# All eight experts in unsplit float32 on quarters of TensorE's columns, with the split buffers as landing buffers

## The chip, the cores and the metric

The kernel runs on one core of one Trainium2 chip. The metric is device time in microseconds of one execution. Three runs of the kernel before gave 3044.08 (median), 3042.06 and 3046.80.

## The reference, cut to what matters

A layered network over 256 tokens of width 1024, all in float32: two transformer layers (attention mixers, then a dense feed-forward in the first and a mixture of experts in the second), and behind them two more layers of another form. The change touches the mixture of experts alone:

```python
logits = xt @ w_router                     # 256 tokens, 8 experts
top_v, top_e = lax.top_k(logits, 2)        # each token goes to two experts
gates = softmax(top_v)
for e in range(8):                         # on the tokens routed to e
    y[e] = (silu(x @ w1[e]) * (x @ w3[e])) @ w2[e]     # w1, w3: 1024 x 3584, w2: 3584 x 1024
out[token] += gate * y[e][token]
```

So there are 512 token slots in all. With the reference's own inputs the experts get 78, 76, 73, 69, 66, 64, 45 and 41 of them. The weights of one expert are 44 MB, of all eight 352.3 MB, and every one is read.

## The kernel before, in words

The program has three stages on one time line: the first layers (two half-batches of 128 tokens as two interleaved threads, `run_pair`), the experts (`moe`), and the last layers (`run_pair` again). All weights come through one `Stream`: a list of loads in order of use, issued by the SP queue (`load`, L333) into raw buffers of 8 KB a partition, of which there are `RAW_BUFS` = 5. A load is one megabyte, 128 partitions by 8 KB.

Float32 matmuls are made of three faster ones. Each half of a raw buffer is split (`need`): ScalarE rounds it to the matmul's fast format (`wh`, L369), VectorE writes the remainder (`wl`, L370), each into one of `SPLIT_BUFS` = 5 buffers of 4 KB; once both halves of the raw buffer are split it is free and the next load may be issued (`free`). `Thread.gemm` then issues for each 128 rows `xh*wh`, `xh*wl` and `xl*wh` (L420 to L422), with 128 tokens stationary and 512 weight columns moving.

Experts are ranked by their token count while the kernel runs; the five largest (`BIG`) get 128 slots and this split form (`expert128`). The three smaller ones get 64 slots and go unsplit (`expert64`, `gemm_pair`, L439): the array's columns are taken as four quarters of 32, two for the slots' two halves with one weight chunk (`w1`) and two with another (`w3`), so that the four quarters work side by side on raw float32 buffers. Such a matmul is two instructions in the trace. A smaller expert's load consists of two pieces of half a megabyte, one from each weight. The two sequences run merged (`run_merged`): units of smaller experts are spread between those of larger ones, from the twelfth load of the stage to the twentieth before its end.

The inner columns of an expert go in seven blocks of 512. Per block, the activation (ScalarE) and the product (VectorE) give `h`, which PE transposes some units later (`defer`, `Tplain` or `T`) into the stationary operand of the last product. That one's output `y` is split in two parts and scattered back to token order by matmuls with a one-hot matrix (`scp`), and `add_rows` (L1621) adds it to the residual with the gate's weight on VectorE. The rows of the next expert are fetched by an indirect DMA on the POOL queue (`gather`, `gather64`) by a side generator that makes a step every second unit. Behind the last expert come statistics (L1626) and the norm.

The first load of an expert can't be issued before routing has written its number to a register (`routing`, `reg`). `overflow` is a branch that is entered only where an expert has more tokens than its slots; it then reads all weights again. The order of instructions on each engine is made by a scheduler from priorities and dependencies, save where the kernel asks for program order.

Of the kernel before, what the change touches and what calls it, by code (L numbers as in the profile page):

```python
# [37 lines left out]
GATHER_AT = 3  # L38
GATHER_AT64 = 2
GATHER_WAIT = 8  # L40
# [7 lines left out]
SMALL_FROM = 12  # L48
SMALL_TO = 20
SPLIT_LEAD = 2.0  # L50
# [85 lines left out]
def weight_plan():  # L136
# [13 lines left out]
    for i in range(2):  # L150
# [17 lines left out]
        if i == 0:  # L168
            for ci, (a, b) in enumerate(chunks(2816)):
                add(("f1", ci), "dense_w1", (0,), a, b)  # L170
                add(("f3", ci), "dense_w3", (0,), a, b)
            full("f2", "dense_w2", (0,), D)
        else:
            for e in range(8):
                for ci in range(7):
                    add((e, "e1", ci), "expert_w1", (0, e), ci * 512, ci * 512 + 512)
                    add((e, "e3", ci), "expert_w3", (0, e), ci * 512, ci * 512 + 512)
                full((e, "e2"), "expert_w2", (0, e), D)
# [26 lines left out]
def weight_groups(shapes):  # L205

    out = []
    end = {}  # L210
    for key, name, idx, c0, c1 in weight_plan():
        kc = shapes[name][-2] // P
# [12 lines left out]
def packed_weights(h):  # L225
# [3 lines left out]
    for key, name, idx, c0, n, kc, groups in plan:  # L229
# [4 lines left out]
    return packs  # L234


def chunk_loads(name, n, kc, groups):
# [3 lines left out]
    for at, k, rows in groups:  # L241
        units = [(kk, min(per, rows - kk), k + kk, n, kc, kk + per >= rows) for kk in range(0, rows, per)]
        out.append(([(name, at, rows, 0, rows, n)], units))
    return out


def pair_loads(chunks):

    out = []
    kc = chunks[0][2]  # L250
    for g, (_, k, rows) in enumerate(chunks[0][3]):
        for j in range(0, rows, 2):
            out.append(([(name, gr[g][0], rows, j, 2, n) for name, n, _, gr in chunks],
                        [(None, 2, k + j, 512, kc, True)]))
    return out


class Stream:


    def __init__(self, m):
# [7 lines left out]
        self.owed = 0  # L269
        self.hold = None  # L270
# [8 lines left out]
    def add(self, key, name, n, kc, groups):  # L279
        assert key not in self.index  # L280
        for pieces, units in chunk_loads(name, n, kc, groups):
            self.loads.append((pieces, None))
            for u in units:
                self.unit(key, len(self.loads) - 1, *u)

    def add_experts(self, one):

        big, small = [], []
        for r in range(8):
            if r < BIG:  # L290
                for k, (name, n, kc, groups) in one.items():
                    big += [((r,) + k, r, pieces, units) for pieces, units in chunk_loads(name, n, kc, groups)]
            else:
                for ci in range(8):
                    ab = [one["e1", ci], one["e3", ci]] if ci < 7 else [one["e2", 0], one["e2", 1]]
                    small += [((r, ci), r, pieces, units) for pieces, units in pair_loads(ab)]
        step = (len(big) - SMALL_FROM - SMALL_TO) / len(small)
        work, load = [], []
        for i, x in enumerate(big):
            load.append((i - SPLIT_LEAD, x))  # L300
            work += [(i + j / len(x[3]), x, u) for j, u in enumerate(x[3])]
        for i, x in enumerate(small):
            load.append((SMALL_FROM + i * step, x))
            work += [(SMALL_FROM + i * step, x, u) for u in x[3]]
        li = {}
        for _, x in sorted(load, key=lambda a: a[0]):
            li[id(x)] = len(self.loads)
            self.loads.append((x[2], x[1]))
        self.hold = len(self.splits) + 1
        for _, x, u in sorted(work, key=lambda a: a[0]):  # L310
            self.unit(x[0], li[id(x)], *u)

    def load(self, parts=1):
        if self.next_load == len(self.loads):
            return
        li = self.next_load
        pieces, rank = self.loads[li]
        if rank is not None and rank not in self.m.expert:
            self.owed += 1
            return  # L320
        self.next_load += 1
        r = self.m.praw.tile([P, 2048], F32, name="raw", tag="raw")
        for i, (name, at, rows, j0, lk, n) in enumerate(pieces):
            v = r[:, i * lk * n:(i + 1) * lk * n].rearrange("p (k n) -> p k n", k=lk)
            if rank is None:
                src = self.m.I[name][at:at + P * rows * n].rearrange("(p k n) -> p k n", p=P, k=rows)
            else:
                w = self.m.I[name].rearrange("(e q) -> e q", e=8)
                src = w[bass.ds(self.m.expert[rank], 1), at:at + P * rows * n].rearrange(
                    "a (p k n) -> p (a k) n", p=P, k=rows)  # L330
            q = lk // parts
            for j in range(0, lk, q):
                self.m.nc.sync.dma_start(v[:, j:j + q], src[:, j0 + j:j0 + j + q])  # L333
        self.raw[li] = r if len(pieces) > 1 else v

    def pay(self):
        n, self.owed = self.owed, 0
        for _ in range(n):
            self.load()

    def start(self):
        for _ in range(RAW_BUFS - 1):
            self.load()
# [8 lines left out]
    def need(self, idx):  # L352
        m = self.m
        nc = m.nc
        while self.next_split <= min(idx, len(self.splits) - 1):
# [5 lines left out]
            if li not in self.raw or j == self.hold:  # L361
# [18 lines left out]
    def free(self, li):  # L380
        del self.raw[li]
        self.load()


class Thread:
# [40 lines left out]
    def gemm_pair(self, key, xT):  # L426

        m = self.m
        ps = m.aux(name="pair")
        for s in m.stream.index[key]:  # L430
            yield s
            li, _, sk, k0, n, kc, _ = m.stream.splits[s]
            w = m.stream.raw[li].rearrange("p (c k n) -> p c k n", c=2, k=sk)
            for j in range(sk):
                k = k0 + j
                x = xT(k)
                for c, h in ((1, 0), (1, 1), (0, 0), (0, 1)):
                    p = c * 64 + h * 32
                    i = m.nc.tensor.matmul(ps[p:p + 32, :n], x[:, h * 32:h * 32 + 32], w[:, c, j, :], start=(k == 0),  # L439
                                           stop=(k == kc - 1))  # L440
                    m.tc.keep_in_program_order(i)
            m.stream.free(li)
            self.tick()
        return ps
# [7 lines left out]
class Model:  # L452
# [115 lines left out]
    def run_merged(self, gens):  # L568

        cur = [next(g, None) for g in gens]  # L570
        while any(c is not None for c in cur):
            i = min((c, i) for i, c in enumerate(cur) if c is not None)[1]
            self.stream.need(self.stream.ahead(cur[i], SPLIT_BUFS - 2))
            self.stream.next_use = cur[i] + 1
            self.side_tick()
            cur[i] = next(gens[i], None)

# [81 lines left out]
    def Tplain(self, src, cols, width, dst, on_act):  # L659
# [3 lines left out]
        for j, c in enumerate(cols):  # L663
            nc.tensor.transpose(tp[:width, j, :], c, self.ident)  # L664
# [15 lines left out]
    def plan(self):  # L680
        S = self.stream = Stream(self)
        self.expert = {}
        one = {}
        for key, name, idx, c0, n, kc, groups in weight_groups(SHAPES)[0]:
            if not name.startswith("expert_"):
                S.add(key, name, n, kc, groups)
            elif idx[1] == 0:
                one[key[1:] if key[1] in ("e1", "e3") else ("e2", key[1])] = (name, n, kc, groups)
                if ("e2", 1) in one:
                    S.add_experts(one)  # L690


    def setup(self):
# [18 lines left out]
        self.stream.start()  # L712
# [9 lines left out]
    def setup_side(self):  # L722
# [95 lines left out]
        for j in range(3):  # L818
# [4 lines left out]
            self.dpart.append(d)  # L823
        yield
# [587 lines left out]
    def routing(self):  # L1412
# [48 lines left out]
        reg(0)  # L1461
        self.stream.pay()
        for r in range(BIG, 8):
            reg(r)
        for r in range(1, BIG):
            reg(r)
# [22 lines left out]
        nc.vector.tensor_scalar(out=cr[:, :BIG], in0=cr[:, :BIG], scalar1=-64.0, scalar2=None, op0=OP.add)  # L1489
# [5 lines left out]
        yield from self.gather(0)  # L1495
        self.stream.hold = None
# [7 lines left out]
    def gather(self, r):  # L1504
# [3 lines left out]
        s = self.st([P, 2, P], name="oh")  # L1508
        self.onehot(s, self.iota, lambda t: self.rtab[:, 0, t, r:r + 1], lambda t: self.rtab[:, 1, t, r:r + 1])
        yield  # L1510
        tp = self.aux((P, 4, P), name="ohp")
        for t in range(2):
            nc.tensor.transpose(tp[:, t, :], s[:, t, :], self.ident)
        sT = self.kvt([P, 2, P], F32R, name="ohT")
        xg = []
        if r == 0:
            gp = []
            for c in range(2):
                p = self.aux((P, 4, P), name="gp")
                for j in range(4):  # L1520
                    k = c * 4 + j
                    for t in range(2):
# [635 lines left out]
```

## Time and profile before

| | |
|---|---|
| median of the runs | 3044.08 us |
| the profiled execution | 3046.54 us |
| its span, first to last instruction | 3044.5 us |
| PE, VectorE, ScalarE busy in the span | 2949.0, 1957.1, 1533.4 us |
| bytes read from memory | 716.87 MB |

The profile's slices are fortieths of the span, 76 us each, with the busy share of each engine in tenths; PE's share comes from modelled ends and is no measure of its peak. The span's last instruction is the output's store, and the time of the execution lies 2.0 us above the span.

### The profile page before, as it was taken

How to read it: one execution, taken by the hardware profiler on the slowest of the kernel's cores; microseconds unless marked ns; L12 is line 12 of the kernel's file. 1: busy time of each engine (PE TensorE's matmuls, PEld its weight loads, DVE VectorE, ACT ScalarE, POOL GpSimd, SP SyncE). 2: the span in 40 equal slices, each digit the busy share in tenths (PEclk: the TensorE clock that was granted, in tenths of full speed). 3: DMA queues.
4: the chain of work that ended last, by engine and by line, in shares of the span. 5: the costliest groups of instructions: out<-in, count | busy, mean ns of one | idle time of the engine just before them, and what ended most of it. 6: DMA issues, size and time to landing. Idle time of an engine off the chain costs nothing. (4 is left out here: it accounts for less than half of the span.)

```text
span 3044.5 us, 40303 instructions
## 1 busy us (share of the span) xinstructions
PE 2949.0 (97%) x15216; PEld 2234.7 (73%) x15216; DVE 1957.1 (64%) x3240; ACT 1533.4 (50%) x2161; POOL 28.4 (1%) x47
## 2 busy tenths in 40 slices
PE   8999999999999999999999899999999999999998
PEld 6887887888655555555555688888888888888887
DVE  6877555777765565656555865757865655668655
ACT  4665444664654444544444644564454444654543
POOL 0000000000000000000000000000000000000000
PEclk9999999999999999999999999999999999999999
DMA  6445555442999999999999855545555555555552
GB/s 226 164 156 185 181 180 172 165 157 87 359 369 367 366 382 369 356 388 367 370 379 375 332 194 180 198 164 183 178 182 190 184 182 194 180 172 175 181 192 97
DMA packets 123048, 721.65 MB, mean 237 GB/s; under 512 B 13976, under 2 KB 14240, under 8 KB 55904
## 3 DMA queue, kind: packets, MB, share of 16 engines
q1 hardware_dynamic: 118368, 703.54, 63.6%
q0 software_dynamic: 4480, 15.48, 1.5%
q8 instruction: 121, 1.98, 0.3%
q14 instruction: 79, 0.65, 0.1%
HBM read 716.87 MB, written 2.10 MB: 236 GB/s over the span
## 5 line engine op out<-in xcount | busy, mean ns | idle before, releaser
L370 DVE TENSOR_TENSOR wl<-raw,wh 128x1024 fp32r<-128x1024 f32 (+1 forms) x1088 | 1299.8, 1215 | 689.9 <-ACT wh L369 686.5
L369 ACT CAST wh<-raw 128x1024 fp32r<-128x1024 f32 (+1 forms) x1088 | 1113.1, 1045 | 849.7 <-PE mm L422 709.4
L420 PE MATMUL mm<-wh,tg 128*128 128x512 f32 (+2 forms) x2928 | 1144.6, 391 | 1.5 <-ACT wh L369 1.0
L421 PE MATMUL mm<-wl,tg 128*128 128x512 f32 (+2 forms) x2928 | 1124.3, 384 | 15.3 <-DVE wl L370 15.0
L422 PE MATMUL mm<-wh,tg 128*128 128x512 f32 (+2 forms) x2928 | 1126.2, 385 | 0.0
L422 PEld LDWEIGHTS mm<-wh,tg 128*128 128x128 f32 x2928 | 552.1, 189 | 131.6 <-issue 24.3
L421 PEld LDWEIGHTS mm<-wl,tg 128*128 128x128 f32 x2928 | 553.3, 189 | 127.3 <-DVE wl L370 25.5
L420 PEld LDWEIGHTS mm<-wh,tg 128*128 128x128 f32 x2928 | 552.7, 189 | 107.3 <-ACT wh L369 5.9
L421 PE MATMUL mm<-wl,xe 128*128 128x512 f32 x560 | 227.7, 407 | 30.9 <-DVE wl L370 29.5
L420 PE MATMUL mm<-wh,xe 128*128 128x512 f32 x560 | 224.1, 400 | 4.7 <-ACT wh L369 4.5
L422 PE MATMUL mm<-wh,xe 128*128 128x512 f32 x560 | 228.2, 407 | 0.0
L421 PEld LDWEIGHTS mm<-wl,xe 128*128 128x128 f32 x560 | 105.5, 188 | 80.2 <-DVE wl L370 51.8
L439 PE MATMUL pair<-raw,xs 128*32 128x512 f32 x1344 | 161.6, 598 | 0.0
L422 PEld LDWEIGHTS mm<-wh,xe 128*128 128x128 f32 x560 | 105.4, 188 | 69.7 <-issue 52.0
L420 PEld LDWEIGHTS mm<-wh,xe 128*128 128x128 f32 x560 | 105.7, 189 | 34.3 <-ACT wh L369 13.3
L643 ACT CAST tg<-tp 128x512 fp32r<-128x512 f32 (+1 forms) x127 | 64.7, 515 | 125.2 <-PE tp L637 124.4
L644 DVE TENSOR_TENSOR tg<-tp,tg 128x512 fp32r<-128x512 f32 (+1 forms) x127 | 75.4, 598 | 43.7 <-ACT tg L643 41.5
L439 PEld LDWEIGHTS pair<-raw,xs 128*32 128x32 f32 x1344 | 35.1, 109 | 80.2 <-issue 80.2
L439 PE MATMUL pair<-raw,hT 128*32 128x512 f32 x672 | 80.8, 598 | 0.0
L1688 DVE TENSOR_TENSOR h<-sl,pair 64x512 f32<-64x512 f32 x21 | 14.5, 691 | 88.5 <-ACT sl L1687 88.5
L1687 ACT ACTIVATE sl<-pair 64x512 f32<-64x512 f32 x21 | 12.4, 590 | 113.9 <-PE pair L439 113.9
L1640 DVE TENSOR_TENSOR h<-sl,mm 128x512 f32<-128x512 f32 x35 | 24.0, 686 | 69.1 <-PE mm L422 68.8
(391 smaller groups left out, 1879.9 us busy)
## 6 DMA issues: line engine op xcount, KB each, us to landing
raw<-in_expert_w_dram SPq DMA_DIRECT2D x210, 1024.0 KB, 7.7
raw<-in_expert_w_dram SPq DMA_DIRECT2D x252, 512.0 KB, 7.0
raw<-in_w_in_dram SPq DMA_DIRECT2D x101, 1024.0 KB, 4.8
raw<-in_ffn_w_in_dram SPq DMA_DIRECT2D x88, 1024.0 KB, 4.8
raw<-in_ffn_w_out_dram SPq DMA_DIRECT2D x40, 1024.0 KB, 4.8
raw<-in_dense_w_dram SPq DMA_DIRECT2D x32, 1024.0 KB, 4.8
raw<-in_w_out_dram SPq DMA_DIRECT2D x16, 1024.0 KB, 4.8
raw<-in_w_branch_diff_dram SPq DMA_DIRECT2D x8, 1024.0 KB, 4.7
```

The lines of the kernel that those rows point to most:

```text
L369: i1 = nc.scalar.copy(hv, src)
L370: i2 = nc.vector.tensor_tensor(out=lv, in0=src, in1=hv.bitcast(F32), op=OP.subtract)
L420: nc.tensor.matmul(o, xh, wh[:, j, :], start=(k == 0), stop=False)
L421: nc.tensor.matmul(o, xh, wl[:, j, :], start=False, stop=False)
L422: nc.tensor.matmul(o, xl, wh[:, j, :], start=False, stop=(k == kc - 1))
L439: i = m.nc.tensor.matmul(ps[p:p + 32, :n], x[:, h * 32:h * 32 + 32], w[:, c, j, :], start=(k == 0), stop=(k == kc - 1))
L643: nc.scalar.copy(hi, tp[:, :nk, :])
L644: nc.vector.tensor_tensor(out=lo, in0=tp[:, :nk, :], in1=hi.bitcast(F32), op=OP.subtract)
L1640: nc.vector.tensor_tensor(out=h, in0=sl, in1=ps, op=OP.mult)
L1687: nc.scalar.activation(sl[64:P, :], ps[0:64, :], AF.Silu)
L1688: nc.vector.tensor_tensor(out=h[odd * 64:odd * 64 + 64, :], in0=sl[64:P, :], in1=ps[64:P, :], op=OP.mult)
```

## The change

All eight experts go unsplit on quarters of the columns. Their weights are packed beforehand as one array `experts` of 8 x 42 units; a unit is one megabyte, 8 KB a partition, that holds two row blocks of 128 and both products' 512 columns (units 0 to 27 pair `w1` with `w3`, units 28 to 41 the two halves of `w2`).

The five larger experts have 96 slots in place of 128: 64 as the smaller ones, and 32 in a second accumulator, where the four quarters take two row blocks of two weights (`ps2`). The partial sums of the two row blocks are added on the way out (on ScalarE and VectorE), and for the last product by the scatter. The smaller experts keep 64. The two sequences are no longer merged: larger and smaller take turns in `ORDER`, so that the last two are both larger.

Odd units land in the split buffers, which the stage no longer needs for splits, from the point where all splits before the experts are made; even units land in the raw buffers. To that end the two split buffers of a unit become one of 8 KB. `fill` issues loads until no buffer of the next one's kind is left. The gathers fetch rows in halves and quarters, the scatters of the last product are put off by two and three units, and the overflow branch is written anew for 96 and 64 slots, in two passes.

```diff
-GATHER_AT = 3
-GATHER_AT64 = 2
-GATHER_WAIT = 8
+GATHER_AT = 2
+GATHER_WAIT = 5
 MA_EVERY = (2, 2)
...
-SMALL_FROM = 12
-SMALL_TO = 20
-SPLIT_LEAD = 2.0
+ORDER = (0, 5, 1, 6, 2, 7, 3, 4)
+UNITS = 42
...
+    def add_experts(self):
+
+        self.experts_from = len(self.splits)
+        for r in ORDER:
+            for u in range(UNITS):
+                ci = min(u // 4, 7)
+                self.loads.append((u, r))
+                self.unit((r, ci), len(self.loads) - 1, None, 2, 2 * (u - 4 * ci), 512, 8 if ci < 7 else 28, True)
+
+    def split_pool(self, li):
+        return self.loads[li][1] is not None and self.loads[li][0] % 2 == 1
 
...
+        what, rank = self.loads[li]
+        w = self.split_pool(li)
+        if self.held[w] == (SPLIT_BUFS if w else RAW_BUFS) or rank is not None and rank not in self.m.expert:
+            return False
+        if w and self.next_split < self.experts_from:
+            return False
         self.next_load += 1
+        self.held[w] += 1
+        if w:
+            r = self.m.pw.tile([P, 2048], F32, name="raww", tag="w")
+        else:
+            r = self.m.praw.tile([P, 2048], F32, name="raw", tag="raw")
...
+            src = self.m.I["experts"][bass.ds(self.m.expert[rank], 1), what].rearrange("a p n -> p (a n)")
+            self.m.nc.sync.dma_start(r, src)
+        self.raw[li] = r
+        return True
...
-            h = m.pw.tile([P, 1024], F32R, name="wh", tag="wh")
-            l = m.pw.tile([P, 1024], F32R, name="wl", tag="wl")
-            hv = h[:, :sk * n].rearrange("p (k n) -> p k n", k=sk)
-            lv = l[:, :sk * n].rearrange("p (k n) -> p k n", k=sk)
+            w = m.pw.tile([P, 2, 1024], F32R, name="w", tag="w")
+            hv = w[:, 0, :sk * n].rearrange("p (k n) -> p k n", k=sk)
+            lv = w[:, 1, :sk * n].rearrange("p (k n) -> p k n", k=sk)
...
+    def gemm_slots(self, key, x64, x32=None):
+        ps = m.pmm.tile([P, 512], F32, name="mm", tag="mm")
+        ps2 = m.aux(name="mm32") if x32 is not None else None
...
+                x = x64(k)
+                for c in (1, 0):
+                    for h in range(2):
+                        mm(ps, c * 64 + h * 32, x[:, h * 32:h * 32 + 32], c, j, k == 0, k == kc - 1)
+            if ps2 is not None:
+                for j in range(sk):
+                    for c in range(2):
+                        mm(ps2, (2 * j + c) * 32, x32(k0 + j), c, j, k0 == 0, k0 == kc - 2)
...
+            if big:
+                q = ci % 4
+                if q == 0:
+                    h2 = self.st([P, 512], name="h2")
+                    if ci == 4:
+                        nc.gpsimd.memset(h2[96:P, :], 0.0)
+                a = self.st([P, 512], name="part")
+                nc.scalar.copy(a[0:64, :], ps2[64:P, :])
+                nc.vector.tensor_tensor(out=a[0:64, :], in0=ps2[0:64, :], in1=a[0:64, :], op=OP.add)
+                sl = self.st([P, 512], name="sl")
+                nc.scalar.activation(sl[32:64, :], a[0:32, :], AF.Silu)
+                nc.vector.tensor_tensor(out=h2[q * 32:q * 32 + 32, :], in0=sl[32:64, :], in1=a[32:64, :], op=OP.mult)
+                if q == 3 or ci == 6:
+                    later(3, h2, h2T[:, ci // 4].rearrange("p q c n -> p q (c n)"))
...
+        for p in (yield from th.gemm_slots((r, 7), *hk)):
+            if p is not None:
+                y = self.A([P, 2, 512], F32R, name="y")
+                nc.scalar.copy(y[:, 0, :], p)
+                nc.vector.tensor_tensor(out=y[:, 1, :], in0=p, in1=y[:, 0, :].bitcast(F32), op=OP.subtract)
+                ys.append(y)
...
+            for i, (y, sT) in enumerate(zip(ys, sTs)):
+                for j in range(2):
+                    self.tc.keep_in_program_order(nc.tensor.matmul(
+                        p, sT[:, c, t, :], y[:, j, :], start=(i + j == 0), stop=(i == len(ys) - 1 and j == 1)))
...
-            th.defer(lambda c=c, t=t: scatter(c, t), 1 + n // 2)
+            th.defer(lambda c=c, t=t: scatter(c, t), 2 + n // 2)
+        if side is not None:
+            self.drain(side)
```

## Rows read from the trace of the kernel before

**Rows 1.** The page's slices: busy tenths of PE and DMA, and the rate.

```profile
PE   8999999999999999999999899999999999999998
...
DMA  6445555442999999999999855545555555555552
GB/s 226 164 156 185 181 180 172 165 157 87 359 369 367 366 382 369 356 388 367 370 379 375 332 194 180 198 164 183 178 182 190 184 182 194 180 172 175 181 192 97
```

**Rows 2.** Stretches: length, busy us of PE, PEld, DVE, ACT, POOL, clock, DMA share, GB/s.

```profile
762.00:790.00 28.00, 25.43 (x119) 19.78 (x120) 22.83 (x31) 18.57 (x23) 1.02 (x1) 0.94 0.98 401
...
815.00:1665.00 850.00, 797.38 (x4330) 457.79 (x4323) 491.25 (x504) 404.68 (x468) 10.46 (x12) 1.00 0.98 371
...
762.00:1718.00 956.00, 897.75 (x4793) 534.63 (x4794) 578.08 (x597) 473.99 (x548) 11.48 (x13) 1.00 0.97 370
...
1070.00:1095.00 25.00, 23.96 (x135) 13.62 (x134) 14.24 (x14) 11.06 (x12) 0.00 (x0) 1.00 1.01 410
```

**Rows 3.** Waits of the DMA queue, 760 to 1720: total us, times, longest.

```profile
SPq L333 <- DVE wl L370: 400.5, 154, 6.5
SPq L333 <- PE pair L439: 266.3, 123, 4.1
```

**Rows 4.** Groups by line and shape, 767 to 1742: busy, mean ns, idle before.

```profile
L369 ACT CAST wh<-raw 128x1024 fp32r<-128x1024 f32 x423 | 420.1, 1050 | 126.1 <-DMA raw<-in_expert_w_dram 99.9 <-PE mm L422 14.5 <-PE pair L439 6.0
...
L637 PE MATMUL tp<-c,h 128*128 128x128 f32 x140 | 22.1, 280 | 7.4 <-DVE h L1640 7.4
...
L1688 DVE TENSOR_TENSOR h<-sl,pair 64x512 f32<-64x512 f32 x21 | 14.5, 691 | 88.5 <-ACT sl L1687 88.5
L1687 ACT ACTIVATE sl<-pair 64x512 f32<-64x512 f32 x21 | 12.4, 590 | 113.9 <-PE pair L439 113.9
```

**Rows 5.** Timeline at the stage's two edges: start, us, engine and line.

```profile
760.57 54.28 SPq L333 DMA_DIRECT2D raw<-in_expert_w_dram  x23
...
767.34 0.39 PE L420 MATMUL mm<-wh,xe 128*128 128x512 f32 x1
...
1739.91 0.39 PE L422 MATMUL mm<-wh,tg 128*128 128x512 f32 x1
...
1741.70 0.73 PE L1658 MATMUL scp<-y,ohT 128*128 128x512 f32 x2
...
1743.04 1.40 DVE L1621 SCALAR_TENSOR_TENSOR z<-scp,rtab,z 128x512 f32<-128x512 f32 x2
...
1744.36 1.39 DVE L1626 BATCH_NORM_STATS2 xbs<-z 128x6 f32<-128x256 f32 x4
...
1745.90 0.26 DVE L1819 BATCH_NORM_AGGREGATE mv<-xbs 128x2 f32<-128x24 f32 x1
```

**Rows 6.** DMA from 760 to 1720: queue share; issues with median us to landing.

```profile
q0 software_dynamic: 1184, 4.19, 1.3%
...
raw<-in_expert_w_dram SPq DMA_DIRECT2D x209, 1024.0 KB, 7.7
raw<-in_expert_w_dram SPq DMA_DIRECT2D x252, 512.0 KB, 7.0
```

**Rows 7.** Timeline of PE over one unit of a smaller expert, by narrow windows.

```profile
1004.00 1.92 PE L439 MATMUL pair<-raw,xs 128*32 128x512 f32 x16
...
1004.46 1.04 PE L439 MATMUL pair<-raw,xs 128*32 128x512 f32 x8
...
1004.89 1.04 PE L439 MATMUL pair<-raw,xs 128*32 128x512 f32 x8
...
1005.86 0.50 PE L422 MATMUL mm<-wh,xe 128*128 128x512 f32 x1
```

**Rows 8.** Timeline of PE behind a wait in the expert stage.

```profile
785.93 0.63 PE L421 MATMUL mm<-wl,xe 128*128 128x512 f32 x1 [0.77 <-DVE wl L370]
786.36 0.63 PE L422 MATMUL mm<-wh,xe 128*128 128x512 f32 x1
```

More of the change, by code (lines that the diff above doesn't have):

```diff
@@ L173, in weight_plan @@
         else:
[L174 to L178, printed above, removed]
+            add(None, None, None, 0, 0)
     for l in range(2):
@@ L242, in chunk_loads @@
         units = [(kk, min(per, rows - kk), k + kk, n, kc, kk + per >= rows) for kk in range(0, rows, per)]
[L243 to L254, printed above, removed]
+        out.append(((name, at, rows, n), units))
     return out
@@ L280, in add @@
         assert key not in self.index
-        for pieces, units in chunk_loads(name, n, kc, groups):
-            self.loads.append((pieces, None))
+        for load, units in chunk_loads(name, n, kc, groups):
+            self.loads.append((load, None))
             for u in units:
                 self.unit(key, len(self.loads) - 1, *u)
[L286 to L311, printed above, removed]
@@ L316, in load @@
         li = self.next_load
[L317 to L320, printed above, removed]
-        self.next_load += 1
[L322 to L343, printed above, removed]
+        what, rank = self.loads[li]
[3 more added lines that the diff above has]
+        if w and self.next_split < self.experts_from:
+            return False
@@ L345, in ahead, with fill @@
+        self.raw[li] = r
+        return True
+    def fill(self):
+        while self.load():
+            pass
     def ahead(self, j, n):
@@ L360, in need @@
                 continue
-            if li not in self.raw or j == self.hold:
+            if li not in self.raw:
                 return
@@ L381, in free @@
         del self.raw[li]
-        self.load()
+        self.held[self.split_pool(li)] -= 1
+        self.fill()
 class Thread:
@@ L682, in plan @@
         self.expert = {}
-        one = {}
-        for key, name, idx, c0, n, kc, groups in weight_groups(SHAPES)[0]:
-            if not name.startswith("expert_"):
+        for chunk in weight_groups(SHAPES)[0]:
+            if chunk is None:
+                S.add_experts()
+            else:
+                key, name, idx, c0, n, kc, groups = chunk
                 S.add(key, name, n, kc, groups)
[L687 to L690, printed above, removed]
     def setup(self):
@@ L1494, in routing @@
         yield
-        yield from self.gather(0)
-        self.stream.hold = None
+        yield from self.gather_first()
     def onehot(self, s, io, pos, sel):
@@ new lines, in gather_first @@
+        gp = []
+        for c in range(2):
+            p = self.aux((P, 4, P), name="gp")
+            for j in range(4):
+                k = c * 4 + j
+                for t in range(2):
+                    nc.tensor.matmul(p[:, j, :], self.XM[t][:, k * P:(k + 1) * P], s[:, t, :], start=(t == 0),
+                                     stop=(t == 1))
+            gp.append(p)
+            yield
+        nc.scalar.copy(x[:, 0:4, :], gp[0])
+        nc.vector.tensor_copy(x[:, 4:8, :], gp[1])
+        self.sT0 = []
@@ new lines, in slots, with slots_first, gather @@
+        return tp, sT
+    def slots_first(self):
+        for n in self.parts_of(0):
+            _, sT = yield from self.slots(0, n)
+            self.sT0.append(sT)
+            yield
+    def gather(self, r):
+        nc = self.nc
+        xs, sTs, rows = [], [], []
+        for n in self.parts_of(r):
+            tp, sT = yield from self.slots(r, n)
+            sTs.append(sT)
+            w = self.st([P, 2, P], name="tokw")
+            for t in range(2):
+                nc.vector.scalar_tensor_tensor(out=w[:, t, :], in0=self.iota, scalar=float(t * P), in1=tp[:, t, :],
+                                               op0=OP.add, op1=OP.mult)
+            tf = self.sm(1, name="tokf")
+            nc.vector.tensor_reduce(out=tf, in_=w.rearrange("p t n -> p (t n)"), axis=AX.X, op=OP.add)
+            ti = self.sm(1, I32, name="toki")
+            nc.vector.tensor_scalar(out=ti, in0=tf, scalar1=float(n), scalar2=self.part[n][2], op0=OP.mult, op1=OP.add)
+            rw = self.A([P, D // n], F32, name="rows")
+            nc.gpsimd.indirect_dma_start(out=rw, out_offset=None,
+                                         in_=self.xrows[:, :].rearrange("t (h n) -> (t h) n", h=n),
+                                         in_offset=bass.IndirectOffsetOnAxis(ap=ti[:, 0:1], axis=0))
+            rows.append(rw)
+            yield
@@ L1663, in expert128 @@
[L1663 to L1678 removed]
+            ps, ps2 = yield from th.gemm_slots((r, ci), *xs)
             odd = ci % 2
@@ new lines, in one_expert @@
+            if ci == GATHER_AT and nxt is not None:
+                side = self.side(self.gather(nxt), GA_EVERY)
+        hk = [lambda k: hT[k // 16][:, k // 8 % 2, k % 4, k // 4 % 2, :]]
+        if big:
+            hk.append(lambda k: h2T[:, k // 16, k % 4, k // 4 % 4, :])
+        ys = []
+        for p in (yield from th.gemm_slots((r, 7), *hk)):
[4 more added lines that the diff above has]
+                ys.append(y)
@@ L1778, in overflow @@
-                for ci in range(4):
-                    ps = prod("expert_w2", 3584, ci * 256, lambda k: hT[k // 8][:, k % 8, :])
-                    nc.scalar.copy(y, ps[:, :256])
-                    for t in range(2):
-                        p = self.aux(name="scp")
-                        nc.tensor.matmul(p[:, :256], sT[:, t, :], y, start=True, stop=True)
-                        z = self.XA[t][:, ci * 256:(ci + 1) * 256]
-                        nc.vector.scalar_tensor_tensor(out=z, in0=p[:, :256], scalar=tb[:, 4 + t:5 + t], in1=z,
-                                                       op0=OP.mult, op1=OP.add)
+                for u in range(2):
+                    self.further(e, io[u], tb, s, rows, xg, sT, hT, wr, sl, h, y, turn)
@@ L2143, in build @@
     host.update(packed_weights(host))
+    host["experts"] = packed_experts(host)
+    for n in ("expert_w1", "expert_w2", "expert_w3"):
+        del host[n]
     host.update(host_constants())
```

327 lines of the change are left out of this document (125 added, 202 removed).

## The prediction

> **What bounds the kernel now.** I read first the page's slices [rows 1]: the reader is to see that the span falls into three parts. In the first ten and the last seventeen slices the DMA engines are about half busy and PE is the full one; in the thirteen between, the experts, the DMA row stands at 9 and the rate doubles. The change lies almost wholly in that middle, so the rest is taken as fixed, and the question is what ends the middle. The stretches by themselves [rows 2] say it: from 815 to 1665 us DMA is at a share of 0.98 with 371 GB/s, while VectorE and ScalarE have 491 and 405 us of 850. PE is listed as 797 busy, but that row models overlapping ends, so I count PE's work in starts (below). The third view is who waits: the DMA queue stands 400 us for VectorE's half of a split (which frees a raw buffer) and 266 us for the quarter matmuls [rows 3], while ScalarE's half stands 100 us for landings of expert weights [rows 4]. So the loads bound the stage, with five landing buffers that leave about 3% of DMA time unfilled, and the split chain is what hands the buffers back. The edges come from the timelines [rows 5]: the first expert load is issued at 760.6, the first expert matmul starts at 767.3, the last scatter at 1741.7, the norm behind the experts at 1745.9. The time that the change can touch is the stretch from 760.6 to 1745.9.
>
> **The loads.** Bytes stay: 8 experts x 42 units x 1.0486 MB = 352.3 MB. Before, 252 of the issues are half-megabyte pieces [rows 6]; after, all 336 are whole ones, and ten buffers take them in place of five, each handed back by the matmuls themselves. What rate follows is not in the trace, so I bound it. Lowest: 370 GB/s at 0.97, what the whole stretch has now [rows 2]. Highest: 410, the best 25 us row. The nearest row is 762 to 790, nearly only whole megabytes into empty buffers: 401 at 0.98. The mixed stretch filled to a share of 1 would give 371/0.98 = 379. I take 395, nearer to the whole-megabyte row, since later rows carry PE reads beside them. Gathers, broadcasts and instruction fetches are some 4.5 MB more (the software queue's 1.3% of the engines, [rows 6], and a little): 356.8 MB / 395 = 903 us, 112.9 an expert, 2.69 a unit.
>
> One rule of the Trainium skill speaks against this: its page "DMA: Bandwidth & Descriptors", section "Specifications", puts the HBM side at about 358 GB/s for one core, below the port ceiling of 435, and loads from HBM should meet the lower one. By it the loads would take 997 us and the kernel some 3070. The trace disagrees over 850 us with 371 [rows 2]; but that a limit sits close above today's rate, wherever it is, is why the rival of an unchanged rate gets more than a token chance.
>
> **PE.** A smaller expert's unit today is 16 instructions from 1004.00 to the next kind's start at 1005.86 [rows 7]: four groups of four, which run side by side on the quarters of the columns. Two groups make one round (all slots of 64, one row block of both products); the groups in the middle start at 1004.46 and 1004.89, 0.43 apart. So a round costs 0.86 among its own kind and up to 0.93 with the change to the full array included (1.86 / 2). After the change nearly all neighbours are of the same kind: I take 0.86 and keep 0.93. A larger expert's unit becomes three rounds (two for 64 slots, one in which two row blocks of the other 32 slots share the array), a smaller one's stays two.
> - Larger: 42 x 3 x 0.86 = 108.4. Beside it six sets of four transposes, those of the next gather, and 16 scatter matmuls: 34 x 0.28 + 16 x 0.36 = 15.4 if nothing overlapped [rows 4, 5]; these durations overlap their neighbours, so 10. Sum 118.4 (with 0.93: 127.2).
> - Smaller: 42 x 2 x 0.86 = 72.2, and 6: 78.2.
>
> All eight: 592 + 235 = 827 us, under the 903 of the loads. The 423 splits of the stage and their waits go (1050 ns each on ScalarE [rows 4], a little more on VectorE), but these are beside the path now; what they free is the raw buffers, sooner. What is late next is the load itself.
>
> **Evictions.** A larger expert's column block now needs two chains: as before one activation and one product, and for the 32 slots a copy, an addition, an activation and a product, about 2 x 0.59 + 2 x 0.69 = 2.6 us [rows 4] and the hops. They have a block's four units, 10.3 us of PE, and their transposes are put two or three units later (5 to 8 us), so PE doesn't wait: nothing. If that cover failed, a wait of 1 us in each of 35 blocks would be 35 us in the larger experts.
>
> **In order.** Loads begin to move at 762. A larger expert eats slower than the loads come (118.4 against 112.9) and lets a lead grow by 5.5; the smaller one behind it eats it up and waits. So six experts, larger and smaller in turn, end by the loads: 762 + 6 x 112.9 + 4 (the last landing, its two rounds) = 1443.4. The last two are both larger and go by PE: + 236.8 = 1680.2. The ten buffers hold 27 us of loads, more than the lead of 11, so the queue isn't stopped on the way. At the very start the split buffers come free only as the stage before them is consumed up to 767: 0 to 5 us; 762 has 1.5 of it.
>
> **The tail.** Before, from the end of the last product to the norm it is 1745.9 - 1740.3 = 5.6. After, four scatters rather than two are open at the end: two evictions of two parts, then on VectorE 4 x 0.70 for the sums and 8 x 0.35 for the statistics [rows 5], 5.6, behind some 3 of product end, evictions and first scatter: 8.7. The norm comes at 1688.9 in place of 1745.9: -57.0. Behind it nothing changes: the next stage's first loads lie in the raw buffers as before, its first splits wait for split buffers that the last odd units free, and the norm gives them time. Outside the stage a split pair now shares one buffer, so VectorE's half is freed with ScalarE's, one matmul later: 0 to 10 us, taken as 0.
>
> Span 3044.5 - 57 = 2987.5; the profiled execution has 2.0 around its span (3046.54) and lies 2.5 above the median of the runs, 3044.08; so 2987 in their terms.
>
> **Rivals.**
> - The rate doesn't rise, since the limit is the memory side and not the number of buffers. For: DMA is already at 0.98, and its queue is rarely empty (a load takes 7.7 us to land [rows 6], about three others' time). Against: rows of 401 and 410. Then 119.5 an expert (956 / 8): 762 + 8 x 119.5 + 4 + 8.7 = 1731, gain 15: 3029.
> - The quarters cost the clock. In a smaller expert PE now works 1.72 us of each 2.69 and waits the rest, 42 times on end. For: the granted clock was 0.94 from 762 to 790 [rows 2], and there the matmuls behind waits start 0.43 us apart and last 0.63 [rows 8] in place of 0.39 [rows 5]: 1.2 GHz, half of the other level; and no stretch of quarter matmuls longer than one unit exists in the trace. Against: from 815 to 1665 the clock is 1.00, though PE stands idle for 53 of the 850 us [rows 2]. If smaller experts ran at 1.2 GHz throughout: 152 each, PE alone would need 767.3 + 592 + 457 + 8.7 = 1825, 79 later: 3123. It turns slower than before once a smaller expert passes 126 us. [...]
> - It doesn't do what it says: with an expert of over 96 tokens the overflow branch would run all weights again, twice, some 16 x 119 us. From the reference's own inputs the experts have 78, 76, 73, 69, 66, 64, 45 and 41 tokens, so it is not entered.
>
> **Numbers.** The forecast 0.60, with its own range: 410 GB/s gives 82 us less, 2962; rounds of 0.93 cost 2 x 8.8 more, 3005; 381 GB/s gives 3012; so 2960 to 3015. Better than that 0.06. Rate unchanged 0.15. Clock 0.08. Overflow 0.01, some other slip (splits late behind the stage) 0.04 slower, 0.06 within the bound. A measurement of this kernel tells about 0.2%, 6 us, from no change. Faster 0.81, same 0.06, slower 0.13. The range goes from 2945 to 3040, which leaves out the slower cases and a little below.
>
> **What would show it.** The stretch from first expert load to the norm near 928 us in place of 985; DMA share 0.99 or more at 390 to 400 GB/s in its steady part; no splits there; PE full in larger experts, about two thirds in smaller, waiting for landings; quarter groups 0.43 apart; the clock at 1.00. Wrong: a rate that stays at 371, a granted clock under 1 in the smaller experts, PE waiting on ScalarE or VectorE in larger ones, or an end of the stage after 1720.

## The result

The changed kernel takes 2950.16 us (2948.08 to 2951.07), the kernel before 3044.86 us beside it: a ratio of 0.9689 [0.9672, 0.9706], 94.7 us less. The forecast was 2987, so direction and mechanism held and the kernel is 37 us faster than forecast. In the profiled executions the span went from 3044.5 to 2947.5 us. All of that lies in the expert stage: its first load is issued at 757.02 (before: 760.57), the norm behind it comes at 1648.94 in place of 1745.90 [rows 5], 97.0 earlier, and the span is 97.0 shorter.

### The profile page after: what moved, and what is told of

Its sections match the earlier page's. It is cut to its first block, busy times and chain, and to the rows that moved or that the text cites. A ratio compares the mean times of both kernels' runs of the same rounds, so it can differ in the third digit from the quotient of the medians.

```text
span 2947.5 us, 43898 instructions
## 1 busy us (share of the span) xinstructions
PE 2872.3 (97%) x17758; PEld 1946.5 (66%) x17758; DVE 1502.5 (51%) x2877; ACT 1171.3 (40%) x1820; POOL 35.9 (1%) x61
## 5 line engine op out<-in xcount | busy, mean ns | idle before, releaser
L354 DVE TENSOR_TENSOR w<-raw,w 128x1024 fp32r<-128x1024 f32 (+2 forms) x668 | 808.8, 1212 | 572.1 <-ACT w L353 570.4
L405 PE MATMUL mm<-w,tg 128*128 128x512 f32 (+2 forms) x2648 | 1033.1, 390 | 0.1
L407 PE MATMUL mm<-w,tg 128*128 128x512 f32 (+2 forms) x2648 | 1013.0, 383 | 0.0
L406 PE MATMUL mm<-w,tg 128*128 128x512 f32 (+2 forms) x2648 | 1012.0, 382 | 0.6 <-DVE w L354 0.6
L353 ACT CAST w<-raw 128x1024 fp32r<-128x1024 f32 (+2 forms) x668 | 695.5, 1043 | 721.6 <-PE mm L407 694.7
L407 PEld LDWEIGHTS mm<-w,tg 128*128 128x128 f32 x2648 | 499.1, 188 | 97.6 <-DVE tg L631 1.2
L405 PEld LDWEIGHTS mm<-w,tg 128*128 128x128 f32 x2648 | 500.2, 189 | 90.9 <-issue 1.7
L406 PEld LDWEIGHTS mm<-w,tg 128*128 128x128 f32 x2648 | 500.5, 189 | 89.7 <-DVE w L354 2.1
L423 PE MATMUL mm<-raw,xs 128*32 128x512 f32 x2352 | 273.9, 594 | 7.1 <-DMA raw<-in_experts_dram 3.8
L423 PE MATMUL mm<-raww,xs 128*32 128x512 f32 x2352 | 273.8, 594 | 7.0 <-DMA raww<-in_experts_dram 7.0
L423 PEld LDWEIGHTS mm<-raww,xs 128*32 128x32 f32 x2352 | 73.6, 110 | 177.8 <-issue 156.8
L423 PEld LDWEIGHTS mm<-raw,xs 128*32 128x32 f32 x2352 | 73.0, 110 | 173.3 <-issue 161.9
L423 PE MATMUL mm<-raw,hT 128*32 128x512 f32 x896 | 107.1, 595 | 12.4 <-DMA raw<-in_experts_dram 10.4
L423 PE MATMUL mm<-raww,hT 128*32 128x512 f32 x896 | 107.1, 596 | 9.3 <-DMA raww<-in_experts_dram 9.3
## 6 DMA issues: line engine op xcount, KB each, us to landing
raw<-in_experts_dram SPq DMA_DIRECT2D x168, 1024.0 KB, 17.7
```

The lines of the kernel that those rows point to most:

```text
L353: i1 = nc.scalar.copy(hv, src)
L354: i2 = nc.vector.tensor_tensor(out=lv, in0=src, in1=hv.bitcast(F32), op=OP.subtract)
L405: nc.tensor.matmul(o, xh, wh[:, j, :], start=(k == 0), stop=False)
L406: nc.tensor.matmul(o, xh, wl[:, j, :], start=False, stop=False)
L407: nc.tensor.matmul(o, xl, wh[:, j, :], start=False, stop=(k == kc - 1))
L423: m.tc.keep_in_program_order(m.nc.tensor.matmul(out[p:p + 32, :], x, w[:, c, j, :], start=start, stop=stop))
```

## The profile after

The page's slices of the changed kernel, the rows that answer to [rows 1]:

```profile
PE   8999999999998998998999899999999999999998
...
PEclk9999999999999999999999999999999999999999
DMA  6445554443799999999999555455555555455552
GB/s 234 158 162 173 188 187 177 146 173 125 304 419 420 420 420 420 419 416 420 419 405 384 188 183 193 171 182 179 174 184 186 188 179 207 166 172 182 181 185 100
```

The full stretch of DMA is over one slice sooner, and within it the rate is a flat 420 GB/s, where it wandered from 356 to 388 before. The dips of PE are the three smaller experts. Stretches of the same kernel (columns as in [rows 2]): the steady part, then a stretch of a smaller expert, of a larger one, and of the last one (also larger).

```profile
800.00:1500.00 700.00, 663.81 (x5814) 203.46 (x5806) 106.60 (x193) 96.83 (x173) 17.45 (x24) 1.00 1.01 419
...
1375.00:1400.00 25.00, 18.03 (x152) 3.93 (x144) 0.00 (x0) 0.00 (x0) 0.00 (x0) 1.00 1.01 420
...
985.00:1060.00 75.00, 75.00 (x677) 23.46 (x677) 17.33 (x29) 16.36 (x28) 1.99 (x3) 1.00 1.01 420
...
1525.00:1625.00 100.00, 100.00 (x896) 32.32 (x892) 17.38 (x25) 16.10 (x27) 1.04 (x2) 1.00 0.96 376
```

The loads run at 419 to 420 whether PE waits (18.03 of 25 us busy) or is full, until the last expert, where all buffers are full and PE takes the lead (376). The clock is 1.00 in each. Waits from 757 to 1640 (total us, times, longest), first PE's whole list, then the DMA queue's three longest:

```profile
PE mm L423 <- DMA raww<-in_experts_dram: 16.3, 29, 1.0
PE mm L423 <- DMA raw<-in_experts_dram: 14.2, 21, 2.0
PE mm L423 <- ACT sl L1624: 3.3, 5, 0.7
PE mm L423 <- ACT y L1651: 2.0, 3, 0.7
...
SPq L322 <- PE mm L423: 415.8, 225, 4.2
SPq L322 <- DMA raww<-in_experts_dram: 117.5, 69, 3.1
SPq L322 <- DMA raw<-in_experts_dram: 113.6, 70, 3.4
```

PE waits for loads, almost never for an eviction. The queue's 400 us for VectorE's splits [rows 3] are gone; it now waits for the quarter matmuls to hand a buffer back, or for an older load to land. The loads of that stretch (count, KB, median us from issue to landing; before in [rows 6]):

```profile
raw<-in_experts_dram SPq DMA_DIRECT2D x168, 1024.0 KB, 17.7
raww<-in_experts_dram SPq DMA_DIRECT2D x168, 1024.0 KB, 17.9
```

17.8 us at 420 GB/s is 7.5 MB under way. Before it was 7.7 us at 371, 2.9 MB: of five buffers some three were loading, while the others lay in the chain of splits. That difference is what most of the experiments are about. Last, the edges, with a unit of a larger and one of a smaller expert (start, us, engine and line; before in [rows 5] and [rows 7]):

```profile
757.02 0.36 SPq L322 DMA_DIRECT2D raw<-in_experts_dram  x1
...
763.75 2.34 PE L423 MATMUL mm<-raw,xs 128*32 128x512 f32 x18
...
1392.63 1.92 PE L423 MATMUL mm<-raw,hT 128*32 128x512 f32 x16 [0.56 <-DMA raw<-in_experts_dram]
1395.12 1.92 PE L423 MATMUL mm<-raww,hT 128*32 128x512 f32 x16 [0.57 <-DMA raww<-in_experts_dram]
...
1631.94 1.90 PE L423 MATMUL mm<-raw,hT 128*32 128x512 f32 x16
...
1633.65 1.04 PE L423 MATMUL mm<-raw,h2T 128*32 128x512 f32 x8
...
1634.51 1.90 PE L423 MATMUL mm<-raww,hT 128*32 128x512 f32 x16
...
1637.20 4.77 PE L1659 MATMUL scp<-y,ohT 128*128 128x512 f32 x16
...
1638.91 2.36 DVE L354 TENSOR_TENSOR w<-raw,w 128x1024 fp32r<-128x1024 f32 x2 [0.25 <-ACT w L353]
...
1641.85 1.22 DVE L354 TENSOR_TENSOR w<-raw,w 128x1024 fp32r<-128x1024 f32 x1
...
1646.92 1.22 DVE L354 TENSOR_TENSOR w<-raw,w 128x1024 fp32r<-128x1024 f32 x1
...
1648.94 0.39 DVE L1777 BATCH_NORM_AGGREGATE mv<-xbs 128x2 f32<-128x24 f32 x2
```

A larger unit takes 1634.51 - 1631.94 = 2.57 us, three rounds of 0.857. A smaller one has two rounds and then waits: 1395.12 - 1392.63 = 2.49, the time of one load (1.0486 MB / 420 GB/s = 2.50). Cut by their matmuls (24 to a larger unit, 16 to a smaller), the experts take, from the first on: larger 114.5, smaller 97.4, larger 116.3, smaller 97.2, larger 116.3, smaller 97.3, larger 117.6, larger 116.4.

## Experiments

Why did the rate rise by 13%? Theory A: a load needs four or more whole megabytes under way to fill the DMA engines, and before only three were, because the split chain held the other buffers. Theory B: the splits of VectorE and ScalarE, which stream the same weights through the same on-chip memory, slowed the transfers. Theory C: it is the pieces, since half of the issues before were half megabytes. Each run was timed beside the kernel before on the same chip, and its ratio is to that.

**The queue cut to five (e1_five).** In `load`:

```
+        if rank is not None and self.held[w] >= (2 if w else 3):
+            return False
```

> Changed kernel with its loads of experts held to five buffers (three raw, two split buffers) in place of ten. Theory A (the rate rose from 371 to 420 GB/s because seven loads stand in the queue instead of three, so that no DMA engine runs dry and no packet starts cold): the DMA share and the rate in the smaller experts fall back to 370 to 395 GB/s; 40 to 66 us longer, 2990 to 3017. Theory B (the rate rose because the splits' reads and writes on ScalarE and VectorE are gone): the rate stays at 415 to 420 GB/s wherever PE waits for loads; only the lead that a larger expert can build is lost, about 22 us, 2972. Theory C (whole megabytes instead of halves): as B.

2948.22 us, ratio 0.9686 [0.9672, 0.9701]. The rate was 419 and loads landed after 17.7 us, as in the changed kernel: the count orders the program only, and the loads are issued as soon as a buffer is free, so the edit changed nothing that the trace shows. It tells nothing of either theory; the runs with fewer buffers below ask the question again.

**The splits' traffic put back (e2_traffic).** Per unit, one made-up split into spare tiles (a second for each fourth unit), 420 in all:

```
+            c = m.c1[:, None, 0:512].to_broadcast([P, 2, 512])
+            for _ in range(2 if s % 4 == 0 else 1):
+                d, e = (m.A([P, 2, 512], F32R, name="d") for _ in range(2))
+                m.nc.scalar.copy(d, c)
+                m.nc.vector.tensor_tensor(out=e, in0=c, in1=d.bitcast(F32), op=OP.subtract)
```

> Changed kernel with 420 made-up splits beside the experts (ScalarE copies 128x1024 from a constant, VectorE subtracts, as the split did; nothing uses them). Theory B (the splits' traffic slowed the loads): rate back to about 370 to 395, some 44 us longer, 2994. Theories A and C: the rate stays at 420 and the time within 6 us of 2950, unless evictions queue behind the made-up work (VectorE some 1.5 us of 2.5 busy).

2950.08 us, 0.9697 [0.9682, 0.9711]. Its steady stretch:

```profile
800.00:1500.00 700.00, 664.19 (x5801) 205.79 (x5793) 498.54 (x539) 422.02 (x515) 44.78 (x22) 0.99 1.01 419
```

VectorE and ScalarE are busier than before (499 and 422 of 700 us, against 491 and 405 of 850 [rows 2]), and the loads still come at 419. Theory B falls, with one limit: the made-up work reads a constant, not the buffers that the loads have just filled.

**Half megabytes (e3_halves).** Each expert load as two issues of 4 KB a partition, in place of one of 8:

```
-            self.m.nc.sync.dma_start(r, src)
+            for c in range(2):
+                self.m.nc.sync.dma_start(r[:, c * 1024:c * 1024 + 1024], src[:, c * 1024:c * 1024 + 1024])
```

> Changed kernel with each load of experts issued as two of half a megabyte (4 KB a partition). Theory C (half-megabyte pieces with 4 KB runs cost the old kernel its rate): rate 380 to 405 GB/s, 20 to 45 us longer, 2971 to 2994. Theories A and B: 415 to 420 GB/s, within 6 us of 2950.

2967.14 us, 0.9750 [0.9735, 0.9765], 17 us of the gain lost. Its steady part, and its loads:

```profile
800.00:1500.00 700.00, 647.86 (x5648) 195.91 (x5644) 104.87 (x191) 93.76 (x168) 17.48 (x24) 1.00 1.03 407
```

```profile
raww<-in_experts_dram SPq DMA_DIRECT2D x336, 512.0 KB, 10.2
```

10.2 us at 407 is 4.2 MB under way, eight halves, and the share of busy time even rises, to 1.03, while 12 GB/s less are carried. Some of the 12 may be that only 4.2 MB are under way, since four whole megabytes carried 414 (the count below); the pieces' own share is then 7 to 12. Theory C holds for that much; in the kernel before only half of the loads were halves.

**Five buffers, and fewer (e6_raw_only, e7_keep1, e7_keep2).** First, expert loads go to the five raw buffers alone, as before the change:

```
     def split_pool(self, li):
-        return self.loads[li][1] is not None and self.loads[li][0] % 2 == 1
+        return False
```

Then one or two of these five are held through the stage by a tile that is written before it and read behind it (`keep`), so that four and three are left.

> Changed kernel in which the experts' loads go to the five raw buffers alone; the split buffers stand empty in the stage. (The earlier run that was to hold the loads to five did not do so: a load takes 17.7 us to land there as in the changed kernel, so seven still stood in the queue.) Theory A (rate by queue depth: below some four outstanding loads engines run dry or start cold): rate in the stage down to 370 to 400 GB/s, 35 to 80 us longer, 2985 to 3030. Theory C (the rate is that of whole megabytes whatever the depth): 415 to 420 GB/s where PE waits, and only the lead is lost: some 22 us, 2972.

> As the run with raw buffers alone, with one of the five held empty through the stage: four. A: rate at or under that of five, 45 to 90 us longer, 2995 to 3040, and a load lands sooner (under 9 us). C: 30 us longer, 2980.

> As the run with raw buffers alone, with two of the five held empty: three, about the depth that the kernel before had in flight. A: rate 330 to 375 GB/s with packets of 8 KB taking 330 ns and more in the mean, 90 to 130 us longer, 3040 to 3080, which would take back the whole gain. C: 37 us longer, 2988.

Five: 2973.16 us, 0.9766 [0.9750, 0.9782], as theory C expected. Four: 2988.57, 0.9818 [0.9801, 0.9834], between the two theories. Three: 3094.1 (3069.97 to 3109.62), 1.0183 [1.0144, 1.0221], slower than the kernel before, if by less than 2%, and beyond even theory A's range; its profile is of the fastest of its runs. With five buffers the first smaller expert and a stretch of the larger one behind it, then the loads:

```profile
880.00:982.00 102.00, 84.78 (x702) 23.82 (x698) 11.31 (x24) 8.80 (x17) 2.48 (x3) 1.00 1.01 415
1000.00:1060.00 60.00, 60.00 (x550) 18.52 (x546) 11.81 (x21) 12.18 (x21) 1.99 (x3) 1.00 1.00 391
...
raw<-in_experts_dram SPq DMA_DIRECT2D x332, 1024.0 KB, 7.8
```

The same with four:

```profile
880.00:985.00 105.00, 84.22 (x694) 23.29 (x689) 11.11 (x23) 8.81 (x17) 2.48 (x3) 1.00 1.00 410
1000.00:1060.00 60.00, 60.00 (x550) 18.44 (x546) 13.40 (x24) 12.94 (x23) 1.99 (x3) 1.00 0.99 380
...
raw<-in_experts_dram SPq DMA_DIRECT2D x325, 1024.0 KB, 7.6
```

With three the steady part, the first smaller expert and a stretch of it, then the loads and PE's wait for them (up to 1640):

```profile
800.00:1500.00 700.00, 584.27 (x4908) 166.01 (x4908) 85.89 (x156) 77.69 (x139) 13.44 (x18) 0.99 0.94 358
885.00:1008.00 123.00, 91.03 (x710) 24.13 (x702) 11.77 (x24) 9.36 (x18) 2.48 (x3) 0.96 0.95 358
925.00:950.00 25.00, 17.56 (x134) 4.33 (x134) 3.30 (x9) 2.51 (x5) 2.48 (x3) 0.93 0.97 374
...
raw<-in_experts_dram SPq DMA_DIRECT2D x298, 1024.0 KB, 6.0
...
PE mm L425 <- DMA raw<-in_experts_dram: 121.2, 121, 3.6
```

In a larger expert PE is the slower, so five or four buffers are soon full and loads wait (391, 380); the five more of the change carry that surplus on: 23 us. In a smaller one PE waits, and the rate is that of the loads: 420 with ten buffers, 415 with five, 410 with four, 358 with three. With three a buffer's turn is 3 x 1.0486 MB / 358 = 8.8 us, of which 6.0 is the load, so on average not three loads are under way but some two.

Loads under way can be counted in the traces: the megabyte loads that are issued and not yet landed, in the smaller experts. With three buffers it is 2.25 in the mean at 355 GB/s, with four 3.1 at 408, with five 4.0 at 414, and with ten 8.0 at 420 (in the run with the larger experts first, below, where every landing can be told). The kernel before, with 2.9 MB under way and 371, lies between the first two. So theory A holds as a slope in the loads under way, steep from two to three and nearly flat from four on, and not in the number of buffers.

Of the 95 us, unsplit weights in the same five buffers give 70.6, the other five buffers 23. The 70.6 were not taken apart: buffers come back after one unit's matmuls instead of a chain of splits, all loads are whole megabytes, and the experts take turns instead of running merged. The kernel before with more buffers or with whole megabytes wasn't tried.

**The order (e5_larger_first, e4_order).** `ORDER` as 0 to 7, all larger experts first, and as 0, 5, 1, 2, 6, 3, 4, 7, with the smaller ones where two larger have filled the buffers.

> Changed kernel with the five larger experts first and the three smaller ones behind. By the sum with the measured 2.50 us a load and 117 us of PE a larger expert: the loads stand full through the larger experts (PE-bound, rate about 370 GB/s) and bound the smaller ones, 18 us longer less 3 for the shorter tail: 2965. If taking turns were worth nothing: 2950.

> Changed kernel with the order larger, smaller, larger, larger, smaller, larger, larger, smaller (ranks 0,5,1,2,6,3,4,7) in place of larger and smaller in turn with two larger at the end. If PE's wait in each smaller expert is what the buffers' lead leaves of the loads, two larger ones in a row build 24 us of lead instead of 12, and the stage should end about 11 us sooner; the tail behind a smaller expert has one eviction and half the scatters less, 2 to 3 us: 2937. If the lead is capped below that (buffers full), 2945 to 2950.

Larger first: 2973.47 us, 0.9773 [0.9757, 0.9789]. A stretch of its larger experts, and one of its smaller:

```profile
900.00:1300.00 400.00, 400.00 (x3560) 126.46 (x3556) 75.31 (x135) 69.56 (x122) 10.81 (x15) 1.00 0.97 375
1400.00:1500.00 100.00, 82.19 (x682) 21.57 (x678) 10.07 (x18) 8.37 (x15) 2.59 (x4) 1.00 1.01 420
```

The loads that full buffers hold up in the one part (375) are missed in the other: taking turns is worth 23 us, where 15 were expected. The other order took 2943.57 us, 0.9673 [0.9660, 0.9686], 6.6 less than the change against an expected 11 to 13. The two were timed again, together on one chip:

> The changed kernel itself, timed again beside the other order of the experts on one chip, so that the two can be told apart: 2950 us again (ratio 0.969 to the kernel before).

> The order larger, smaller, larger, larger, smaller, larger, larger, smaller, a second time, beside the changed kernel on the same chip. If its gain of 6.6 us is real: 2942 to 2945 us, and the intervals of the two ratios stand apart. If it was the difference of two chips: within 2 us of the changed kernel.

The change 2948.56 us (2947.86 to 2949.55), the order 2944.36 (2943.2 to 2945.1): no run of the one lies among the other's, so 4 us are real. (The intervals of the two ratios, 0.9688 [0.9675, 0.9701] and 0.9674 [0.9661, 0.9687], do overlap, against what was expected.) A smaller expert behind two larger ones took 92.3 us in place of 97.4, while its loads alone need 42 x 2.50 = 105: ten buffers give a lead of 13 us, not of 25. That some are always the ones being loaded would explain it; no run shows that alone.

**A larger and a smaller expert in one turn (e9_pairs, e10_pairs_last).** If lead is short, it is better not to need it: four units of the one and four of the other, then their second products.

```
+GROUPS = ((0,), (1, 5), (2, 6), (3, 7), (4,))
...
+            live = [self.one_expert(th, r, nxt if r == g[0] else ()) for r in g]
+            while live:
+                for e in list(live):
+                    for u in e:
+                        if u is None:
+                            break
+                        yield u
+                    else:
+                        live.remove(e)
```

(`one_expert` yields None behind each column block, the loads are listed in the same order, and two more one-hot tiles take the place of one other.) The second kernel has the groups (0,), (1,), (2, 5), (3, 6), (4, 7).

> If what is left after the change is lead: buffers hold only some 13 us of loads (a smaller expert ran 12.6 us under its loads' 105), so a larger expert can't earn all that a smaller one wants. Here a larger and a smaller expert share a turn, four units of the one and four of the other, and their two second products follow one another: a pair needs 194 us of TensorE for 210 us of loads, so nothing has to be kept for long. One larger expert comes first (114.5 us), then three pairs at 198, 210 and 210, then a larger one (117), and a tail of 11.6: the norm at 1620 us against 1648.9, a time of about 2920 us. If instead units of two experts in turn cost TensorE or the buffers more than that (two experts' tiles live at a time, two gathers in one turn), no gain or a loss: 2945 us or more.

> The same with two larger experts first and a pair last, so that the loads and not TensorE end the stage: all loads are 336 x 2.497 = 839 us from 757, done at 1596, and the norm a last unit and a tail later, at about 1610 us: 2910 us, if the two larger experts at the start don't fill all buffers and stop the loads. If they do, the loads that are lost there come back at the end: 1615 to 1622 us, no better than the order with the larger expert last.

2938.46 us, 0.9660 [0.9647, 0.9673], and 2940.2, 0.9668 [0.9655, 0.9682]: both faster than the change, the first by 10 us, and a third of what was expected. The terms of the expectation for the first add up to 1625 and not to the 1620 it gives; the norm came at 1638.9. The first expert took 116.9 (two gathers beside it), the pairs 202.5, 213.5 and 215.4 in place of 198, 210 and 210, the last expert 115.2. The stretches of two pairs and of the last expert:

```profile
1100.00:1500.00 400.00, 378.79 (x3300) 116.06 (x3296) 56.27 (x100) 53.02 (x93) 9.00 (x13) 1.00 1.01 420
1520.00:1600.00 80.00, 80.00 (x727) 24.98 (x723) 15.79 (x23) 16.13 (x27) 1.59 (x3) 1.00 1.01 419
```

The rate now stays at 420 to the end, and the last load is issued at 1601.5 where the change issues it at 1611.6; the norm, too, comes 10 us sooner. The 335 intervals between issues are 2.52 us each, against 2.50 for a megabyte at 420: there is hardly a stop left, so full buffers had cost the changed kernel only these 10 us and not 30. The second kernel loses loads as its own second theory said, for its two larger experts fill the buffers at the start; but its norm comes at 1639.1, not at 1615 to 1622:

```profile
900.00:1100.00 200.00, 200.00 (x1784) 62.94 (x1780) 38.13 (x74) 36.53 (x65) 6.30 (x8) 1.00 0.99 394
```

## Why the prediction was right, and which term was mis-sized

By its own steps, forecast norm 1688.9, measured 1648.9:

- **The loads' rate**, taken as 395 GB/s, was 420: 2.50 us a megabyte. This is the term that was mis-sized. With the same 356.8 MB, 420 gives 106.2 an expert where the sum had 112.9; by the sum's own steps six experts then end at 762 + 6 x 106.2 + 4 = 1403.2 in place of 1443.4, and 1402.7 was measured. That is the 40 us. The step that misled was "the mixed stretch filled to a share of 1 would give 371/0.98 = 379": the share of busy time is no measure of how full the engines are. It was 0.94 with three buffers at 358, 0.98 before at 371 [rows 2], 1.01 at 420 and 1.03 with halves at 407; 358/0.94 would have given 381 as the ceiling. The upper bound, 410 as "the best 25 us row", was a misreading: the kernel before has better ones, so that the rate to come stood in its trace.

```profile
1050.00:1075.00 25.00, 25.00 (x146) 15.19 (x145) 14.80 (x16) 12.27 (x14) 0.00 (x0) 1.00 1.02 418
...
1350.00:1375.00 25.00, 24.65 (x137) 14.71 (x136) 15.07 (x15) 11.58 (x13) 0.00 (x0) 1.00 1.02 414
```

- **The range**: 2960 to 3015 was the forecast's own, and 2950 lies outside it, in the case that had a chance of 0.06. It lies within 2945 to 3040 because that was made wider, by luck as much as by working.
- **Start**: the first issue is 3.6 us earlier than before, which the sum didn't have, and yet its end of six experts agrees within 1 us. Terms of that size offset one another, and no run separates them.
- **Lead**: ten buffers were to hold 27 us of loads; by the run on the order they give some 13. What that cost here is the 10 us that the pairs won back.
- **PE**: a round of 0.857 against 0.86, larger experts at 114.5 to 117.6 against 118.4. Right. The two at the end took 234.5 (forecast 236.8), and went by PE as said.
- **Evictions** hidden: PE's waits for ScalarE are 5.3 us in 880. Right.
- **Tail**: 1648.9 - 1637.3 = 11.6 against 8.7. VectorE's four splits for the next stage, 4.8 us (the 2.36 and two times 1.22 at L354), get between the sums and the statistics; the working had left them out.
- **Behind the stage** nothing changed: stage and span both 97.0 shorter. Right, as the 0 of its range of 0 to 10.

The rivals. The rate doesn't rise: refuted by 420. The clock: refuted at 1.00 in experts that wait 0.56 us of each 2.49, with 2.0 us the longest wait. The rival has its place all the same. With three buffers the granted clock of a stretch in a smaller expert fell to 0.93: in six short spells of that trace PE ran at 1.2 GHz in place of 2.4, each at a wait of 2.1 to 3.1 us. There was one such spell with four buffers, at a wait of 2.5, and three with the made-up splits, at waits of 3.2.

The rule of 358 GB/s a core was the wrong one to weigh: the Trainium skill's page "HBM Reference", section "Specifications (TRN2)", says that a core that streams alone measures about 425, and 358 is a share when two stream. The trace agrees, with 420. That three buffers give 358 here is by the runs with four and more a matter of loads under way, and no limit of the memory.

## What to carry to other kernels

Judge a stream of loads by the bytes under way (time to land x rate) and by its best stretches, not by a DMA share near 1: of whole megabytes, two under way gave some 355 GB/s here, three 408, four 414 and eight 420, so that past four buffers buy lead and hardly any rate. A buffer that holds a load until a chain on other engines is through counts as not there; the step to unsplit weights, whose matmuls hand it back, came with whole megabytes and the taking of turns and was worth more (71 us) than doubling the number of buffers (23 us). Where work that is faster than its loads alternates with work that is slower, take turns: the coarser the turn, the more buffers it needs.

## What the runs showed of the hardware

- Sixteen DMA engines with whole megabytes of 8 KB a partition hold 419 to 420 GB/s over 700 us beside full PE reads; with 4 KB a partition 407, at a higher share of busy time. With fewer whole megabytes under way the rate falls: 414 at 4.0, 408 at 3.1, 355 at 2.25.
- Work of 499 and 422 us in 700 on VectorE and ScalarE, on other tiles than those that are loaded, takes nothing from the loads (419).
- Four float32 matmuls of 128x32 by 128x512 side by side on the quarters of the columns start every 0.43 us a half round, 0.857 a round, for a whole stage, as the single units of before did.
- A queue kept up to eight loads under way, halves (4.2 MB) or whole megabytes (19.6 us x 420 GB/s = 8.2 MB with experts in pairs), and then waited for an older load to land; what sets that number the runs don't show.
